# Two column pairs of the first MLP product in full, an alternating norm and split, one weight pool for both products, and the first chunk fetched earlier

## Chip, cores and metric

The kernel runs on one core of one Trainium2 chip. The metric is the device time of one execution in microseconds (us). Engines are named as in the profile: PE is the matmul engine, PEld its weight loads, DVE the vector engine, ACT the scalar engine, POOL the GpSimd engine, and SP the queue from which most DMAs are issued.

## What is computed

One residual layer on 512 frames of width 2048, all in float32. A first part (one wide projection, attention, a spatial gating unit, a merge and an output projection) gives a new `x`. The change concerns the second part:

```
h2 = rms_norm(x, g_ff)                                     # 512 x 2048
x  = x + square(relu(h2 @ w_ff1)) @ w_ff2                  # w_ff1 2048 x 8192, w_ff2 8192 x 2048
```

## The kernel before

Every product is made in three passes (`mm3`, lines 72 to 74): each operand is split into a high part, rounded to the matmul's format by an ACT cast, and a low part, the rest, by a DVE subtraction. The three matmuls are high by high, high by low and low by high. `split_to` (lines 107 and 108) and `weight` (lines 91 to 96) do this for a tile and for a streamed piece of weights.

The order on each engine is not written out by hand: a scheduler simulates the program and fills each engine's in-order queue with whatever is ready, earlier program text first. `tc.issue_after(ins)` queues what is traced inside it behind `ins` on that engine. Tiles come from pools with a fixed number of buffers; a new tile waits until one is free. When a pool is closed and another opened in its memory, the new tiles wait for the old ones.

**Pools.** `slots` has 64 buffers of 128 x 512 floats (2 KB a partition) and holds nearly everything. `long` has 12 more of that size, `short` 6, `raws` 3 of 128 x 1024 for weights on their way. After the output projection `short` and `raws` close and `raw1` (6 buffers of 128 x 1024) opens in their place. After the first MLP product `long` and `raw1` close, and `raw2` and `more2` (6 each) open. `wpool` holds three pairs of split weight pieces at a time.

**Norm.** After the output projection the transposed rows `x2T[0..15]` (each 128 x 512) are scaled by `rstd_b` on DVE (line 662), and each of their two halves of 256 frames is split (ACT cast at line 107, DVE subtraction at line 108) into `hs["y11"]`, `hs["y12"]` (even `b`) and `hs["y21"]`, `hs["y22"]` (odd `b`), eight tiles of each.

**First product.** `w_ff1` is taken in 32 pairs of column blocks (2 x 128 columns). Pair 0 is made in full (matmuls into `f`): 16 row blocks x 2 column blocks x 2 halves x 3 passes = 192 matmuls of 256 columns, with the weights in four pieces. The other 31 pairs, `hidden(p)`, use a Strassen-like scheme with seven products instead of eight (`NAMES`: y11, y21, m7, m6, y22, m4, m5): 7 x 8 x 3 = 168 matmuls of 256 columns (into `q`). The sums of the activation blocks for m7, m6, m4 and m5 are made once by `factors` (lines 643 to 646, then split): 32 DVE sums, 32 casts and 32 subtractions of 128 x 256. The sums of the weight blocks are made for each pair in `Sums.parts`: three DVE additions (lines 173, 177 and 179) and one that a DMA accumulates (line 175, POOL's queue).

`keep_hidden(p)` squares the two tiles of a pair, makes their seven factors (four sums and seven subtractions on DVE, seven casts on ACT) and stores them in DRAM (line 681, seven stores of 256 KB). In the text it stands right behind each pair.

**Second product.** It goes through eight chunks `f` of 1024 hidden columns, that is of four pairs. For each, `fetch` loads 28 tiles of 256 KB (line 730), four for each name. The outputs are made in two halves `g`, each `strassen_tokens`: seven names x two weight pieces x 12 matmuls of 512 columns. The first piece's weight blocks (`i = 0`) come from pool `state["raw"]`, the second's from `state["more"]`. The results are added to `x2` tiles, loaded again from DRAM at line 741. The tiles of chunk `f + 1` are fetched between the names of chunk `f`; chunk 0 is fetched after the last pair.

Of the kernel before, what the change touches and what calls it, by code (L numbers as in the profile page):

```python
# [2 lines left out]

# [7 lines left out]
F32R = mybir.dt.float32r  # L11
AF = mybir.ActivationFunctionType
# [15 lines left out]
W = 512  # L28
SLOTS = 64
LONG = 12  # L30
SHORT = 6


@with_exitstack
def tile_hybrid_layer(ctx: ExitStack, tc: tile.TileContext, x, g_mix, w_in, g_q, g_k, ln_g, ln_b,
# [8 lines left out]
    small = ctx.enter_context(tc.tile_pool(name="small", bufs=8))  # L44
    slots = ctx.enter_context(tc.tile_pool(name="slots", bufs=SLOTS))
    dram = ctx.enter_context(tc.tile_pool(name="dram", bufs=1, space=bass.MemoryType.DRAM))
    first, before = ExitStack(), ExitStack()
    long = first.enter_context(tc.tile_pool(name="long", bufs=LONG))
    short = before.enter_context(tc.tile_pool(name="short", bufs=SHORT))
    raws = before.enter_context(tc.tile_pool(name="raws", bufs=3))  # L50
    ps_acc = ctx.enter_context(tc.tile_pool(name="ps_acc", bufs=5, space=bass.MemoryType.PSUM))
    ps_aux = ctx.enter_context(tc.tile_pool(name="ps_aux", bufs=3, space=bass.MemoryType.PSUM))

    def slot(name, dt=F32, pool=slots):
        return pool.tile([P, 512], dt, name=name, tag="slot")

    def acc(name):
        return ps_acc.tile([P, 512], F32, name=name, tag="acc")
# [7 lines left out]
    def f32(ap):  # L66
        return ap.bitcast(F32)


    def mm3(o, lh, rh, start, stop, **kw):  # L70

        nc.tensor.matmul(o, lhsT=lh[0], rhs=rh[0], start=start, stop=False, **kw)  # L72
        nc.tensor.matmul(o, lhsT=lh[0], rhs=rh[1], start=False, stop=False, **kw)  # L73
        nc.tensor.matmul(o, lhsT=lh[1], rhs=rh[0], start=False, stop=stop, **kw)  # L74
# [12 lines left out]
    def weight(wap, kt, c0, w=W):  # L87

        ck = CK * W // w
        raw = state["raw"].tile([P, ck, w], F32, name="w_raw", tag="w_raw")  # L90
        state["load"] = nc.sync.dma_start(
            out=raw, in_=wap[kt * P:(kt + ck) * P, c0:c0 + w].rearrange("(k p) c -> p k c", p=P))
        hi = wpool.tile([P, ck, w], F32R, name="w_hi", tag="w_piece", bufs=6)
        nc.scalar.copy(out=hi, in_=raw)  # L94
        lo = wpool.tile([P, ck, w], F32R, name="w_lo", tag="w_piece", bufs=6)
        nc.vector.tensor_tensor(out=lo, in0=raw, in1=f32(hi), op=ALU.subtract)  # L96
        return hi, lo

    def split(src, name, scale=None, pool=slots):

        hi, lo = slot(name + "_hi", F32R, pool), slot(name + "_lo", F32R, pool)
        split_to(hi, lo, src, scale)
        return hi, lo

    def split_to(hi, lo, src, scale=None):
        if scale is None:
            nc.scalar.copy(out=hi, in_=src)  # L107
            nc.vector.tensor_tensor(out=lo, in0=src, in1=f32(hi), op=ALU.subtract)  # L108
        else:
            nc.scalar.activation(out=hi, in_=src, func=AF.Copy, scale=scale)  # L110
            nc.vector.scalar_tensor_tensor(out=lo, in0=src, scalar=scale, in1=f32(hi),
                                           op0=ALU.mult, op1=ALU.subtract)
# [199 lines left out]
    def hT_of(k):  # L312

        if k == len(hT):
            t = aux("xT")
            for tb in range(NTB):
                nc.tensor.transpose(out=t[:, tb * P:(tb + 1) * P], in_=xq[tb, k], identity=ident)
            hT.append(split(t, "hT", gT[:, k:k + 1], long if k < LONG // 2 else short if k < (LONG + SHORT) // 2 else slots))
        return hT[k]

    def scale_of_x():
# [309 lines left out]
    rstd2 = rsqrt(ms2, 4, "rstd2")  # L631
    flush()
    along(rstd2, rstd_b)
    before.close()
    state["raw"] = first.enter_context(tc.tile_pool(name="raw1", bufs=6))


    def factors(ys, act, k):
# [11 lines left out]
    def halves(src, pool=slots):  # L650

        t = slot("ys", F32R, pool)
        split_to(t[:, :HS], t[:, HS:], src)
        return t

    def sides(t):
        return t[:, :HS], t[:, HS:]

    hs = {}
    for b in range(KT):  # L660
        y = x2T[b]
        nc.vector.tensor_tensor(out=y, in0=y, in1=rstd_b, op=ALU.mult)
        for half in range(2):
            name = "y" + "12"[b % 2] + "12"[half]
            far = name == "y11" or name == "y21" and b // 2 < LONG - KT // 2
            hs[name, b // 2] = halves(y[:, half * HS:(half + 1) * HS], long if far else slots)

    GROUP = 4
    chunks = DFF // (GROUP * 2 * P)
# [11 lines left out]
            nc.sync.dma_start(out=store[p // GROUP][i, p % GROUP], in_=f32(ys[name, 0]))  # L681


    o = [acc("f1") for _ in range(2)]
    for kt in range(0, KT, 4):
        hi, lo = weight(w_ff1[0], kt, 0, 2 * P)
        for c in range(2):
            for k in range(4):
                a = [part[:, k, c * P:(c + 1) * P] for part in (hi, lo)]
                for half in range(2):  # L690
                    name = "y" + "12"[k % 2] + "12"[half]
                    mm3(o[c][:, half * HS:(half + 1) * HS], a, sides(hs[name, (kt + k) // 2]),
                        kt + k + half == 0, kt + k == KT - 1, skip_group_check=True)
    act = []
    for c in range(2):
        t = slot("relu")
        nc.scalar.activation(out=t, in_=o[c], func=AF.Relu)
        act.append(t)
    for k in range(KT // 2):
        factors(hs, x2T[2 * k:2 * k + 2], k)  # L700
    keep_hidden(0, act)
    rhs = {name: [sides(hs[name, k]) for k in range(KT // 2)] for name in NAMES}

    def hidden(p):

        act = [slot("relu"), slot("relu")]
        a11, a12, a21, a22 = (act[c][:, half * HS:(half + 1) * HS] for c in range(2) for half in range(2))

        def evac(name, o):
            for a, sign in {"y11": [(a11, 1.0)], "m7": [(a22, 1.0)], "m6": [(a21, -1.0)],  # L710
                            "y22": [(a12, 1.0)]}.get(name, []):
                nc.scalar.activation(out=a, in_=o, func=AF.Copy, scale=sign)  # L712
            for a, op in {"y21": [(a11, ALU.add)], "m4": [(a21, ALU.add)],
                          "m5": [(a22, ALU.subtract), (a12, ALU.add)]}.get(name, []):
                nc.vector.tensor_tensor(out=a, in0=a, in1=o, op=op)

        strassen_columns(w_ff1[0], p * 2 * P, rhs, evac)
        for a in act:
            nc.scalar.activation(out=a, in_=a, func=AF.Relu)
        keep_hidden(p, act)  # L720

    for p in range(1, DFF // (2 * P)):
        hidden(p)

    def fetch(f, name):

        ts = []
        for p in range(GROUP):
            t = slot("ys", F32R)
            nc.sync.dma_start(out=f32(t), in_=store[f][NAMES.index(name), p])  # L730
            ts.append(sides(t))
        return ts

    first.close()
    second = [ctx.enter_context(tc.tile_pool(name=n, bufs=6)) for n in ("raw2", "more2")]
    state["raw"], state["more"] = second
    lhs = {name: fetch(0, name) for name in NAMES}
    for tb in range(NTB):
        for j in range(D // W):
            t = slot("x2")  # L740
# [53 lines left out]
```

## Time and profile before

| | |
|---|---|
| median of 3 runs | 2550.4 us (2548.84 to 2552.09) |
| the profiled execution | 2549.47 us, of which the span of the trace is 2547.8 us |
| PE busy | 2485.3 us, 98% |
| DVE busy | 1608.8 us, 63% |
| ACT busy | 1041.3 us, 41% |
| POOL busy | 205.1 us, 8% |
| mean granted PE clock | 0.988 of full speed |

The page's first part gives each engine's busy time. A matmul counts as busy until its modelled end, so neighbours overlap. The second part cuts the span into 40 equal slices of 63.7 us. In later views a stretch is given by its ends in microseconds from the start of the span.

### The profile page before, as it was taken

How to read it: one execution, taken by the hardware profiler on the slowest of the kernel's cores; microseconds unless marked ns; L12 is line 12 of the kernel's file. 1: busy time of each engine (PE TensorE's matmuls, PEld its weight loads, DVE VectorE, ACT ScalarE, POOL GpSimd, SP SyncE). 2: the span in 40 equal slices, each digit the busy share in tenths (PEclk: the TensorE clock that was granted, in tenths of full speed). 3: DMA queues.
4: the chain of work that ended last, by engine and by line, in shares of the span. 5: the costliest groups of instructions: out<-in, count | busy, mean ns of one | idle time of the engine just before them, and what ended most of it. 6: DMA issues, size and time to landing. Idle time of an engine off the chain costs nothing. (4 is left out here: it accounts for less than half of the span.)

```text
span 2547.8 us, 35037 instructions
## 1 busy us (share of the span) xinstructions
PE 2485.3 (98%) x13634; PEld 2165.9 (85%) x13634; DVE 1608.8 (63%) x2116; ACT 1041.3 (41%) x1517; POOL 205.1 (8%) x186
## 2 busy tenths in 40 slices
PE   8999999999999999999789999999997999999999
PEld 7888888888888888888679999999996788888887
DVE  4555463332335333322788888888875988888887
ACT  4333332222223222222456666666663333333333
POOL 0212110000111010100000000000000000000000
PEclk9999999999999999999889999999998999999999
DMA  5332323333333333344368878888889988767763
GB/s 174 91 86 73 91 67 99 95 96 99 116 92 99 100 99 97 128 143 134 87 168 217 223 214 221 229 228 220 223 231 359 299 253 247 221 209 230 249 178 96
DMA packets 343159, 419.15 MB, mean 165 GB/s; under 512 B 17056, under 2 KB 180944, under 8 KB 342992
## 3 DMA queue, kind: packets, MB, share of 16 engines
q1 hardware_dynamic: 302048, 383.87, 46.6%
q0 software_dynamic: 40944, 33.03, 9.1%
q8 instruction: 107, 1.75, 0.3%
q14 instruction: 60, 0.49, 0.1%
HBM read 349.72 MB, written 67.11 MB: 164 GB/s over the span
## 5 line engine op out<-in xcount | busy, mean ns | idle before, releaser
L107 ACT CAST w_hi<-w_raw 128x1024 fp32r<-128x1024 f32 x441 | 464.5, 1054 | 616.4 <-PE q L73 561.0
L96 DVE TENSOR_TENSOR w_lo<-w_raw,w_hi 128x1024 fp32r<-128x1024 f32 x212 | 263.1, 1241 | 606.2 <-ACT w_hi L94 583.9
L108 DVE TENSOR_TENSOR w_lo<-w_raw,w_hi 128x1024 fp32r<-128x1024 f32 x441 | 538.7, 1222 | 166.1 <-ACT w_hi L107 165.8
L94 ACT CAST w_hi<-w_raw 128x1024 fp32r<-128x1024 f32 x212 | 223.0, 1052 | 683.7 <-PE ga L73 99.6
L72 PE MATMUL q<-ys,w_hi 128*128 128x256 f32 x1736 | 493.0, 285 | 7.3 <-ACT relu L712 3.6
L73 PE MATMUL q<-ys,w_hi 128*128 128x256 f32 x1736 | 492.7, 285 | 6.8 <-DVE ys L108 6.8
L74 PE MATMUL q<-ys,w_lo 128*128 128x256 f32 x1736 | 488.4, 284 | 0.6 <-DVE w_lo L108 0.6
L73 PE MATMUL q<-w_lo,ys 128*128 128x512 f32 x896 | 350.3, 391 | 3.0 <-DVE w_lo L108 3.0
L74 PE MATMUL q<-w_hi,ys 128*128 128x512 f32 x896 | 350.0, 391 | 0.0
L72 PEld LDWEIGHTS q<-ys,w_hi 128*128 128x128 f32 x1736 | 329.1, 190 | 9.0 <-ACT ys L107 4.3
L73 PEld LDWEIGHTS q<-ys,w_hi 128*128 128x128 f32 x1736 | 329.1, 190 | 8.2 <-DVE ys L108 8.1
L72 PE MATMUL q<-w_hi,ys 128*128 128x512 f32 x896 | 315.3, 391 | 17.3 <-DMA ys<-store 16.2
L74 PEld LDWEIGHTS q<-ys,w_lo 128*128 128x128 f32 x1736 | 327.1, 190 | 0.8 <-DVE w_lo L108 0.8
L72 PEld LDWEIGHTS q<-w_hi,ys 128*128 128x128 f32 x896 | 168.9, 189 | 54.4 <-DMA ys<-store 17.1
L73 PEld LDWEIGHTS q<-w_lo,ys 128*128 128x128 f32 x896 | 169.0, 189 | 39.2 <-DVE w_lo L108 4.1
L74 PEld LDWEIGHTS q<-w_hi,ys 128*128 128x128 f32 x896 | 169.0, 189 | 35.1
L175 POOL DMA_DIRECT2D w_raw<-in_w_ff_dram x63 | 86.5, 1373 | 1368.8 <-DVE w_raw L173 659.2
L755 DVE TENSOR_TENSOR x<-x,q 128x512 f32<-128x512 f32 x256 | 167.8, 681 | 10.8 <-PE q L74 7.0
L72 PE MATMUL gb<-hT_hi,w_hi 128*128 128x512 f32 x256 | 100.3, 392 | 0.2 <-DVE gb L454 0.2
L72 PE MATMUL xo<-w_hi,mT_hi 128*128 128x512 f32 x256 | 100.5, 393 | 0.0
L72 PE MATMUL ga<-hT_hi,w_hi 128*128 128x512 f32 x256 | 100.4, 392 | 0.0
L73 PE MATMUL ga<-hT_lo,w_hi 128*128 128x512 f32 x256 | 100.0, 391 | 0.0
(213 smaller groups left out, 4023.8 us busy)
## 6 DMA issues: line engine op xcount, KB each, us to landing
w_raw<-in_w_ff_dram SPq DMA_DIRECT2D x256, 512.0 KB, 4.9
w_raw<-in_w_in_dram SPq DMA_DIRECT2D x144, 512.0 KB, 3.8
store<-ys SPq DMA_DIRECT2D x224, 256.0 KB, 4.9
ys<-store SPq DMA_DIRECT2D x224, 256.0 KB, 5.4
w_raw<-in_w_ff_dram POOLq DMA_DIRECT2D x63, 512.0 KB, 7.0
w_raw<-in_w_out_dram SPq DMA_DIRECT2D x32, 512.0 KB, 3.7
w_raw<-in_w_oa_dram SPq DMA_DIRECT2D x16, 512.0 KB, 3.6
w_raw<-in_w_ob_dram SPq DMA_DIRECT2D x16, 512.0 KB, 3.7
```

The costliest lines, as they stand in the source:

```text
L72: nc.tensor.matmul(o, lhsT=lh[0], rhs=rh[0], start=start, stop=False, **kw)
L73: nc.tensor.matmul(o, lhsT=lh[0], rhs=rh[1], start=False, stop=False, **kw)
L74: nc.tensor.matmul(o, lhsT=lh[1], rhs=rh[0], start=False, stop=stop, **kw)
L94: nc.scalar.copy(out=hi, in_=raw)
L96: nc.vector.tensor_tensor(out=lo, in0=raw, in1=f32(hi), op=ALU.subtract)
L107: nc.scalar.copy(out=hi, in_=src)
L108: nc.vector.tensor_tensor(out=lo, in0=src, in1=f32(hi), op=ALU.subtract)
L175: nc.gpsimd.dma_start(out=self.w21, in_=self.blocks[1, 1], accum_op=ALU.add)
L755: nc.vector.tensor_tensor(out=a, in0=a, in1=o, op=op)
```

## The change

- Pairs 0 and 1 are made in full (`PLAIN = 2`); `factors` stands behind both in the text. Thirty pairs are left for the seven-product scheme.
- `keep_hidden` of pairs 0 and 1 is moved behind pair 2; from there on each pair's stands behind that pair, as before.
- The scaling of `x2T[b]` is queued on DVE behind the last subtraction of `x2T[b - 2]`.
- `raws` now has six buffers and stays open to the end; it serves as `state["raw"]` in every stage. `short` is gone. Three pairs of split input tiles (`hT` 6 to 8) that lay in `short` lie in three of these buffers.
- `long` alone closes behind the first product, and `more` opens in its place.
- `lhs`, the 28 fetches of chunk 0, stands ahead of the last `keep_hidden` in the text, where it stood behind it and behind the pools' change.

```diff
-    short = before.enter_context(tc.tile_pool(name="short", bufs=SHORT))
-    raws = before.enter_context(tc.tile_pool(name="raws", bufs=3))
+    raws = ctx.enter_context(tc.tile_pool(name="raws", bufs=6))
...
+            if LONG // 2 <= k < LONG // 2 + RAWH:
+                both = raws.tile([P, 2, W], F32R, name="hT_both", tag="w_raw")
+                parts = both[:, 0, :], both[:, 1, :]
+                split_to(*parts, t, gT[:, k:k + 1])
...
-    before.close()
-    state["raw"] = first.enter_context(tc.tile_pool(name="raw1", bufs=6))
...
+    order = []
     for b in range(KT):
         y = x2T[b]
-        nc.vector.tensor_tensor(out=y, in0=y, in1=rstd_b, op=ALU.mult)
+        with tc.issue_after(order[b - 2].ins) if b > 1 else nullcontext():
+            nc.vector.tensor_tensor(out=y, in0=y, in1=rstd_b, op=ALU.mult)
...
+        order.append(state["lo"])
...
+    PLAIN = 2
+    acts = []
+    for p in range(PLAIN):
+        o = [acc("f1") for _ in range(2)]
+        for kt in range(0, KT, 4):
+            hi, lo = weight(w_ff1[0], kt, p * 2 * P, 2 * P)
...
+        acts.append(act)
     for k in range(KT // 2):
         factors(hs, x2T[2 * k:2 * k + 2], k)
-    keep_hidden(0, act)
...
-        keep_hidden(p, act)
-
-    for p in range(1, DFF // (2 * P)):
-        hidden(p)
+        return act
...
+    pairs = DFF // (2 * P)
+    for p in range(PLAIN, pairs):
+        acts.append(hidden(p))
+        if p == pairs - 1:
+            lhs = {name: fetch(0, name) for name in NAMES}
+        while acts:
+            keep_hidden(p + 1 - len(acts), acts.pop(0))
+
     first.close()
-    second = [ctx.enter_context(tc.tile_pool(name=n, bufs=6)) for n in ("raw2", "more2")]
-    state["raw"], state["more"] = second
-    lhs = {name: fetch(0, name) for name in NAMES}
+    state["more"] = ctx.enter_context(tc.tile_pool(name="more", bufs=6))
```

## Rows read from the trace of the kernel before

**Rows 1.** The page, its 40 slices: PE's busy tenths, PE's granted clock.

```profile
PE   8999999999999999999789999999997999999999
PEclk9999999999999999999889999999998999999999
```

**Rows 2.** PE's waits over the span: what it waited for, us, times, longest.

```profile
PE q L72 <- DMA ys<-store: 16.2, 2, 15.5
PE f L73 <- DVE ys L108: 6.9, 1, 6.9
PE q L73 <- DVE ys L108: 6.8, 5, 1.7
```

**Rows 3.** Busy time by stretch: length, engines' busy us, PE clock, DMA share, GB/s.

```profile
1218.90:1235.10 16.20, 2.84 (x10) 2.28 (x10) 11.12 (x23) 9.16 (x29) 2.81 (x2) 0.58 0.28 37
1235.10:1259.50 24.40, 24.36 (x191) 24.36 (x192) 18.55 (x41) 6.25 (x11) 0.00 (x0) 0.93 0.08 23
1259.50:1302.40 42.90, 28.33 (x173) 24.91 (x172) 36.46 (x84) 22.79 (x52) 1.60 (x1) 0.76 0.38 104
1302.40:1907.10 604.70, 604.69 (x5040) 604.49 (x5038) 507.81 (x749) 386.63 (x659) 46.18 (x30) 1.00 0.82 222
1907.10:1922.60 15.50, 0.05 (x1) 0.05 (x1) 10.38 (x18) 6.62 (x13) 1.20 (x1) 0.62 0.99 324
1922.60:1967.20 44.60, 42.23 (x166) 33.58 (x167) 24.25 (x27) 13.69 (x13) 0.00 (x0) 0.90 1.04 376
1967.20:2009.20 42.00, 39.59 (x171) 31.57 (x171) 37.34 (x41) 14.67 (x15) 4.81 (x4) 1.00 1.06 346
2009.20:2542.40 533.20, 533.20 (x2353) 441.25 (x2351) 463.60 (x501) 204.78 (x194) 31.01 (x26) 1.00 0.70 212
```

**Rows 4.** DVE in order of time around the norm and the first sums.

```profile
1226.23 8.52 DVE L662 TENSOR_TENSOR x2T<-x2T,rstd_b 128x512 f32<-128x512 f32 x14
1234.67 9.47 DVE L108 TENSOR_TENSOR ys<-x2T,ys 128x256 fp32r<-128x256 f32 x28
...
1246.41 1.42 DVE L108 TENSOR_TENSOR ys<-x2T,ys 128x256 fp32r<-128x256 f32 x4
...
1254.92 1.23 DVE L108 TENSOR_TENSOR w_lo<-w_raw,w_hi 128x1024 fp32r<-128x1024 f32 x1 [4.53 <-ACT w_hi L107]
...
1286.15 0.75 DVE L108 TENSOR_TENSOR ys<-m,ys 128x256 fp32r<-128x256 f32 x2
```

**Rows 5.** PE in order of time: pair 0's stream begins, pair 1's begins.

```profile
1235.14 0.58 PE L73 MATMUL f<-ys,w_hi 128*128 128x256 f32 x1 [6.93 <-DVE ys L108]
...
1259.47 0.28 PE L72 MATMUL q<-ys,w_hi 128*128 128x256 f32 x1
```

**Rows 6.** DMA issues on SP in order of time, around the second product's start.

```profile
1891.29 2.00 SPq L167 DMA_DIRECT2D w_raw<-in_w_ff_dram  x4
...
1903.36 10.05 SPq L167 DMA_DIRECT2D w_raw<-in_w_ff_dram  x6
...
1918.09 0.98 SPq L730 DMA_DIRECT2D ys<-store  x1
...
1921.68 18.92 SPq L730 DMA_DIRECT2D ys<-store  x27
1940.96 10.48 SPq L741 DMA_DIRECT2D x<-kept  x16
1951.81 13.54 SPq L730 DMA_DIRECT2D ys<-store  x20
1965.74 3.75 SPq L167 DMA_DIRECT2D w_raw<-in_w_ff_dram  x6
```

**Rows 7.** ACT in order of time: a cast that waited for weights.

```profile
1971.90 1.05 ACT L107 CAST w_hi<-w_raw 128x1024 fp32r<-128x1024 f32 x1 [5.89 <-DMA w_raw<-in_w_ff_dram]
```

**Rows 8.** Busy time by stretch, as in Rows 3, where the DMAs were fullest.

```profile
1941.00:1952.00 11.00, 9.33 (x40) 7.20 (x39) 5.80 (x7) 2.70 (x3) 0.00 (x0) 1.00 1.05 387
```

**Rows 9.** The page's DMA issues: count, KB each, us from issue to landing.

```profile
store<-ys SPq DMA_DIRECT2D x224, 256.0 KB, 4.9
```

More of the change, by code (lines that the diff above doesn't have):

```diff
@@ L1 @@
 import collections
-from contextlib import ExitStack
+from contextlib import ExitStack, nullcontext
 import concourse.bass as bass
@@ L30 @@
 LONG = 12
-SHORT = 6
+RAWH = 3
 @with_exitstack
@@ L46, in tile_hybrid_layer @@
     dram = ctx.enter_context(tc.tile_pool(name="dram", bufs=1, space=bass.MemoryType.DRAM))
-    first, before = ExitStack(), ExitStack()
+    raws = ctx.enter_context(tc.tile_pool(name="raws", bufs=6))
+    first = ExitStack()
     long = first.enter_context(tc.tile_pool(name="long", bufs=LONG))
-    short = before.enter_context(tc.tile_pool(name="short", bufs=SHORT))
-    raws = before.enter_context(tc.tile_pool(name="raws", bufs=3))
     ps_acc = ctx.enter_context(tc.tile_pool(name="ps_acc", bufs=5, space=bass.MemoryType.PSUM))
@@ L107, in split_to @@
             nc.scalar.copy(out=hi, in_=src)
-            nc.vector.tensor_tensor(out=lo, in0=src, in1=f32(hi), op=ALU.subtract)
+            state["lo"] = nc.vector.tensor_tensor(out=lo, in0=src, in1=f32(hi), op=ALU.subtract)
         else:
@@ L317, in hT_of @@
                 nc.tensor.transpose(out=t[:, tb * P:(tb + 1) * P], in_=xq[tb, k], identity=ident)
-            hT.append(split(t, "hT", gT[:, k:k + 1], long if k < LONG // 2 else short if k < (LONG + SHORT) // 2 else slots))
+            if LONG // 2 <= k < LONG // 2 + RAWH:
+                both = raws.tile([P, 2, W], F32R, name="hT_both", tag="w_raw")
+                parts = both[:, 0, :], both[:, 1, :]
+                split_to(*parts, t, gT[:, k:k + 1])
+            else:
+                parts = split(t, "hT", gT[:, k:k + 1], long if k < LONG // 2 else slots)
+            hT.append(parts)
         return hT[k]
@@ L681, in keep_hidden @@
             nc.sync.dma_start(out=store[p // GROUP][i, p % GROUP], in_=f32(ys[name, 0]))
-    o = [acc("f1") for _ in range(2)]
-    for kt in range(0, KT, 4):
-        hi, lo = weight(w_ff1[0], kt, 0, 2 * P)
-        for c in range(2):
[L688 to L698, printed above, removed]
+    PLAIN = 2
[4 more added lines that the diff above has]
+            hi, lo = weight(w_ff1[0], kt, p * 2 * P, 2 * P)
+            for c in range(2):
+                for k in range(4):
+                    a = [part[:, k, c * P:(c + 1) * P] for part in (hi, lo)]
+                    for half in range(2):
+                        name = "y" + "12"[k % 2] + "12"[half]
+                        mm3(o[c][:, half * HS:(half + 1) * HS], a, sides(hs[name, (kt + k) // 2]),
+                            kt + k + half == 0, kt + k == KT - 1, skip_group_check=True)
+        act = []
+        for c in range(2):
+            t = slot("relu")
+            nc.scalar.activation(out=t, in_=o[c], func=AF.Relu)
+            act.append(t)
+        acts.append(act)
     for k in range(KT // 2):
         factors(hs, x2T[2 * k:2 * k + 2], k)
-    keep_hidden(0, act)
     rhs = {name: [sides(hs[name, k]) for k in range(KT // 2)] for name in NAMES}
```

## The prediction

> **What bounds the kernel now.** I read the slices first. PE is at nine tenths nearly everywhere and at full clock, except in two places: slices 20 and 21 and, later, slice 31 [rows 1]. The list of PE's waits gives them names: 16.2 us for `ys<-store`, the fetch of chunk 0, and 6.9 and 6.8 us for `ys`, the split halves and sums that DVE makes [rows 2]. The stretches then give sizes [rows 3]. From 1218.9 to 1235.1 PE waits for the norm. Pair 0 takes until 1259.5. Pair 1 takes 42.9 us, of which PE works 28.3. Thirty pairs take 604.7, that is 20.16 each, with no wait. Then PE stands for 15.5 us, and the first chunk takes 44.6 + 42.0 = 86.6 us; the other seven take 533.2, 76.17 each. So PE sets the time, and only about 65 us are to be had, at the two changes of stage. In each I look for what ends last.
>
> **Two prices for PE.** A pair is 168 matmuls, so one costs 20.16 / 168 = 0.120 us at full clock. A weight piece of the second product is 76.17 / 28 = 2.72 us.
>
> **The alternating norm.** DVE now makes 14 scalings in 8.52 us (0.609 each) before its first subtraction, at 1234.67; 28 subtractions then take 9.47 (0.338 each) [rows 4], and pair 0 starts at 1235.14 [rows 5]. With the new order two scalings come first, so the first subtraction starts at 1226.23 + 2 x 0.61 = 1227.4, and PE at about 1227.9, 7.2 us sooner. But PE then goes at DVE's pace: one `b` costs 0.609 + 2 x 0.338 = 1.285, and sixteen 20.6. The fourth `b`, with five scalings and eight subtractions, is done at 1226.23 + 5.7 = 1232.0. The 24 matmuls on the first four `b` take up to 24 x 0.24 = 5.8 us at half clock (the stretch before shows 0.58 [rows 3]), until 1233.7. The other 168 at 0.120 take 20.2: pair 0 ends near 1254. Bounds: at the soonest the last `b` comes at 1226.2 + 20.6 = 1246.8 and 30 matmuls follow, 1250.4; if the next 24 run at half clock too, 1256.8. It ended at 1259.5: I take a gain of 5.5 (2.7 to 9).
>
> **Pair 1 in full.** It costs 192 x 0.120 = 23.0 us. What goes is pair 1 as it was, 42.9 us [rows 3], with its waits for sums and its half clock. Gain 19.9, if DVE has the sums of the activations ready for pair 2's third product, m7.
>
> DVE's work from 1226.2: norm and split 20.6; five weight pieces at 1.23 [rows 4], 6.2; the 64 sums and subtractions of `factors`, of the halves' size, at 0.338, 21.6. Together 48.4, so 1274.6. Pair 2 needs DVE for some five operations of 1.23 ahead of m7: 1280.8. PE reaches pair 2 at 1254 + 23 = 1277 and m7 two products (5.8) later, 1282.8, and its last row block some 2.5 later still. That is a cover of 2 to 4.5 us. Against it: DVE's queue is in order, and a low part at its head that waits for a free buffer holds the sums behind it. It did so for 4.53 us at 1254.92 [rows 4], and the last sums came at 1286.15. Then the two postponed `keep_hidden` bring 2 x 11 x 0.338 = 7.4 us. DVE is busy 507.8 / 30 = 16.9 of 20.16 us in a pair [rows 3], and pair 2 runs without the 3.7 us of its predecessor's; so one `keep_hidden` fits there and one is left over, against pieces made up to three products (8.6 us) ahead. I take a loss of 2 us (0 if all is hidden; 10 if two waits like that at 1254.92 fall on the sums). If the cover is gone, m7 of pair 2 is late next.
>
> **The chunk fetched early.** SP issues the 28 fetches behind pair 31's stores, from 1918.09 [rows 6], when PE had been idle since 1907.1. Now 44 of the 64 slots hold activation factors, 13 the last two pairs' tiles, so seven fetches find room when pair 31 begins, and the rest as y21, m7 and m6 are used up. The first four tiles should be there before the pair ends: 15.5 us of standing go. The fetches are moved past seven stores, and what stands behind them (16 `x2` loads, 20 fetches of chunk 1, six weight loads [rows 6]) moves up with them.
>
> The first chunk also lost 86.6 - 76.2 = 10.4 us. Of this the clock is 44.6 x 0.10 = 4.5 [rows 3], which goes with the idle time; the rest is small waits. But the DMAs are full here: share 1.05, 387 GB/s [rows 8]. From 1891.3 on, up to the last six weight loads, SP and POOL issue 2 + 3.5 + 3 + 7 + 4 + 5 + 3 + 1 = 28.5 MiB (14 stores and two accumulating loads included), 29.9 MB or 77 us at 387 GB/s, and the cast that needed the end of them waited until 1971.90 [rows 7]. With one pool for both products the loads can begin as in any pair, at best 8 us sooner: 1883 + 77 = 1960, and 1962.3 with cast (1.05) and subtraction (1.23). PE would begin `g = 1` at 1907.1 + 38.1 = 1945.2; three pieces of it are loaded early, so it misses the fourth at 1953.4. If the order on SP stays, PE stands for about 9 us there; if the six weight loads pass the 20 fetches (5.2 MB, 13.5 us), for none; if the DMAs start no sooner, for 21. I take 6, so 15.5 + 10.4 - 6 = 20 us gained (5 to 26).
>
> [...]
>
> **Edits at no cost.** Six `raws` buffers, three of them taken by `hT`, leave three for the weights of the first part, as before; PE waits for none there (slices 2 to 19 [rows 1]), and at the start at worst three loads of 0.5 MB pass the `x` loads, 4 us, at best they come as much sooner. I take 0. Where the cover is lost, the second slice shows it.
>
> **The sum.** 5.5 + 19.9 - 2 + 20 = 43.4. The profiled execution took 2549.47, so 2506.1; the median is 0.9 above it: **2507 us**. The bounds together: 2.7 + 19.9 - 10 + 5 = 17.6 (2533) and 9 + 19.9 + 26 = 54.9 (2495.5).
>
> **The rivals.**
>
> *A, the DMAs keep the second gain.* SP's order puts chunk 0 late, or the full DMAs move PE's stand to `g = 1`: 23.4 us from the first place, 0 to 10 from the second, 2517 to 2527. For it: share 1.05 over 100 us [rows 3]. Against: seven free slots and 28 fetches with no other condition.
>
> *B, DVE keeps the first gain.* The sums are late in spite of pair 1: 10 us more lost, or more while the backlog lasts, 2515 to 2527. For it: the wait at 1254.92, and 84% of DVE taken in each pair. Against: between 1235.1 and 1302.4 DVE was busy for 18.6 + 36.5 of 67.3 us [rows 3], so 12 are to spare.
>
> *C, slower: the slots.* If the scheduler lets the 28 fetches take slots as soon as chunk 0 is stored, some 27 pairs run without spare slots, and a pair's tiles wait for the landing of the stores before, 4.9 us [rows 9]: 27 x 4.9 = 132 us, about 2640. It decides from 43.4 / 27 = 1.6 us a pair. [...] Against it: seven slots stood free in all 30 pairs, and no tile of chunk 0 was fetched into them before its turn [rows 6].
>
> *D, no change:* the fetches stay in place and DVE's order eats the rest. Both places would have to fail; neither depends on the other.
>
> **Chances.** Forecast (2496 to 2516) 0.66; A 0.13; B 0.12; more gain than the bounds 0.02; D 0.02; C 0.05. The range 2495 to 2530 leaves out C, D and little of A and B. About 0.2% (5 us) is what a measurement of this kernel can tell from none: faster 0.93, within 0.02, slower 0.05.
>
> **What would show it.** Pair 0's first L73 near 1228 and its end near 1254. Pair 2's first matmul near 1277, its m7 without waits on `ys`. The thirty pairs still 20.16 each; one or two longer ones at the beginning would be the backlog. No hole at the end of pair 31, PE's clock at 1.00 there. In `g = 0` to `g = 1` of chunk 0, PE's only wait, on w_hi or w_lo behind a weight DMA. I am wrong if pairs in the middle are longer than 20.2, if L730 still stands behind the last stores, or if chunk 0 takes over 95 us.

## The result and the profile after

The changed kernel takes 2531.9 us (median of 4 runs, 2528.42 to 2533.67) where the kernel before takes 2551.1 beside it: a ratio of 0.9924, 95% interval 0.9907 to 0.9942. The direction was right; of the 43.4 us that were forecast, 19.2 came by the medians. The profiled execution took 2531.66 us (span 2530.0), 17.8 less than before, and the accounts below are of profiled executions.

Line numbers have moved: the three matmuls of a product are L71 to L73, low parts L95 and L107, the sums of `factors` L646 to L649, the relu of the pairs in full L706, fetches L736, `x2` loads L753, the addition onto `x2` L767.

First the slices of the changed kernel, PE's busy tenths and its granted clock; they answer to [rows 1].

```profile
PE   8999999999999999999989999999997999999999
PEclk9999999999999999999989999999998999999999
```

Of the weak spot at slices 20 and 21 only slice 21 is left; that at slice 31 is still there. PE's waits in the changed kernel (us, times, longest), which answer to [rows 2]:

```profile
PE q L71 <- DVE x L767: 6.8, 1, 6.8
PE q L72 <- DVE ys L107: 6.7, 5, 1.7
PE q L71 <- DMA ys<-store: 4.7, 1, 4.7
...
PE q L71 <- ACT ys L106: 2.7, 2, 1.4
...
PE q L71 <- ACT relu L721: 2.0, 1, 2.0
```

The norm's 6.9 us are gone, the store's 16.2 have become 4.7. The five short waits on `ys`, which the sums make, stand as they were: 6.7 after 6.8. And one is new: 6.8 us for an addition onto `x2`. The stretches of the changed kernel, with the columns of [rows 3], say where:

```profile
1222.80:1250.60 27.80, 27.80 (x219) 27.73 (x219) 22.44 (x49) 13.24 (x34) 0.00 (x0) 0.94 0.20 58
1250.60:1271.00 20.40, 20.40 (x172) 20.40 (x171) 9.57 (x10) 7.85 (x11) 1.73 (x1) 1.00 0.30 53
1271.00:1326.00 55.00, 42.36 (x278) 38.72 (x277) 53.14 (x116) 34.73 (x78) 3.11 (x2) 0.82 0.58 173
1326.00:1899.00 573.00, 572.91 (x4765) 572.10 (x4764) 480.89 (x707) 365.17 (x621) 44.26 (x29) 1.00 0.83 224
1899.00:1903.70 4.70, 0.02 (x1) 0.02 (x1) 2.50 (x3) 1.51 (x3) 0.00 (x0) 0.94 1.10 274
1903.70:1952.30 48.60, 40.08 (x159) 31.71 (x160) 27.50 (x37) 16.47 (x21) 0.00 (x0) 0.87 1.05 388
1952.30:1991.00 38.70, 38.67 (x171) 31.65 (x170) 35.82 (x40) 14.67 (x14) 4.59 (x4) 1.00 1.06 358
1991.00:2524.00 533.00, 533.00 (x2353) 441.49 (x2352) 464.93 (x502) 204.73 (x194) 31.22 (x27) 1.00 0.70 213
```

Both pairs in full run without a hole (1222.8 to 1271). Then PE works 42.4 of 55 us at clock 0.82: pair 2 stands where pair 1 stood. In the second of these rows DVE, whose sums PE is about to wait for, works only 9.57 of 20.4 us. Its order of time there (start, length, instruction, idle time before it and what ended it) is this:

```profile
1252.05 1.23 DVE L95 TENSOR_TENSOR w_lo<-w_raw,w_hi 128x1024 fp32r<-128x1024 f32 x1 [4.58 <-ACT w_hi L93]
...
1259.93 1.23 DVE L107 TENSOR_TENSOR w_lo<-w_raw,w_hi 128x1024 fp32r<-128x1024 f32 x1 [2.92 <-ACT w_hi L106]
1265.69 1.22 DVE L107 TENSOR_TENSOR w_lo<-w_raw,w_hi 128x1024 fp32r<-128x1024 f32 x1 [4.53 <-ACT w_hi L106]
1266.94 1.23 DVE L178 TENSOR_TENSOR w_raw<-w_raw 128x1024 f32<-128x1024 f32 x1
1268.09 0.42 DVE L646 TENSOR_TENSOR m<-x2T 128x256 f32<-128x256 f32 x1
...
1296.96 1.42 DVE L107 TENSOR_TENSOR ys<-m,ys 128x256 fp32r<-128x256 f32 x4
```

The first sum, L646, begins at 1268.09 although its operands were there when the norm ended near 1247; the last of the sums' low parts ends at 1298.4. The first sum stands behind weight parts of pairs 1 and 2 (L95 and L107), and those of pair 2 wait for a cast that itself waits for PE to finish with a buffer. ACT shows these casts:

```profile
1258.85 1.05 ACT L106 CAST w_hi<-w_raw 128x1024 fp32r<-128x1024 f32 x1 [4.36 <-PE f L72]
1264.61 1.05 ACT L106 CAST w_hi<-w_raw 128x1024 fp32r<-128x1024 f32 x1 [4.71 <-PE f L72]
```

Before, the same sequence ended in a first sum at 1257.3; [rows 4] has its low part that waited 4.53.

PE in the changed kernel, at the points that answer to [rows 5] and at the begin of the second product:

```profile
1222.38 0.50 PE L71 MATMUL f<-ys,w_hi 128*128 128x256 f32 x2 [1.94 <-ACT ys L106]
...
1270.29 0.28 PE L71 MATMUL q<-ys,w_hi 128*128 128x256 f32 x1
...
1897.28 0.73 PE L71 MATMUL q<-w_hi,ys 128*128 128x512 f32 x2
...
1903.68 0.79 PE L71 MATMUL q<-w_hi,ys 128*128 128x512 f32 x1 [4.74 <-DMA ys<-store]
...
1930.78 0.80 PE L71 MATMUL q<-w_hi,ys 128*128 128x512 f32 x1 [6.84 <-DVE x L767]
```

SP's issues in the changed kernel, which answer to [rows 6], and the addition that PE waited for on DVE:

```profile
1873.60 10.54 SPq L166 DMA_DIRECT2D w_raw<-in_w_ff_dram  x7
...
1887.29 0.32 SPq L736 DMA_DIRECT2D ys<-store  x1
...
1892.48 1.00 SPq L736 DMA_DIRECT2D ys<-store  x2
...
1895.71 22.42 SPq L736 DMA_DIRECT2D ys<-store  x25
...
1922.56 2.57 SPq L753 DMA_DIRECT2D x<-kept  x3
```

```profile
1930.03 1.41 DVE L767 TENSOR_TENSOR x<-x,q 128x512 f32<-128x512 f32 x2 [7.67 <-DMA x<-kept]
```

The fetches do begin before pair 31 ends, but 25 of 28 go out in one block from 1895.71, 1.6 us before the end. Ahead of the first of them SP spends 10.54 us on seven weight loads of the second product; of SP's waits from 1870 to 1900, 10.0 us are of weight loads for buffers that DVE was still reading. The first `x2` tile, which the first addition needs, is issued behind the fetches at 1922.56. The product m6 adds onto y11's PSUM bank, and PE stood for 6.84 us until DVE had taken y11 out.

**An account that closes.** For every run I take three numbers from PE's rows in order of time. *Start* is the first matmul of the pairs in full. *Excess* is the time from there to the end of pair 31 less the matmuls themselves: 23.0 for a pair in full, 20.16 for another (the prices of the prediction). *Chunk 0* is the time from the end of pair 31 to the start of the last matmul, less 533.2 for the seven later chunks [rows 3]; so a later chunk that became longer would count in it.

| kernel | median us | ratio, 95% interval | start | first sum | excess | chunk 0 |
|---|---|---|---|---|---|---|
| before | 2551.1 | | 1227.4 | 1257.3 | 31.7 | 101.8 |
| after | 2531.9 | 0.9924 [0.9907, 0.9942] | 1222.4 | 1268.1 | 24.0 | 93.9 |
| relu_late | 2519.7 | 0.9882 [0.9868, 0.9897] | 1222.8 | 1246.3 | 9.9 | 94.4 |
| plain1 | 2533.2 | 0.9937 [0.9922, 0.9951] | 1226.9 | 1256.0 | 22.7 | 94.5 |
| x2_ahead | 2530.8 | 0.9921 [0.9904, 0.9937] | 1222.9 | 1269.2 | 24.6 | 92.2 |
| fetch_late | 2534.8 | 0.9941 [0.9926, 0.9955] | 1222.7 | 1268.2 | 21.7 | 98.0 |
| no_alt | 2537.1 | 0.9944 [0.993, 0.9959] | 1222.9 | 1276.1 | 28.3 | 94.6 |
| c1_after | 2522.7 | 0.9891 [0.9874, 0.9907] | 1223.0 | 1268.3 | 21.4 | 84.2 |
| combo | 2509.6 | 0.9837 [0.9822, 0.9852] | 1223.8 | 1248.3 | 11.1 | 83.4 |
| plain3 | 2524.4 | 0.9895 [0.988, 0.9909] | 1223.7 | 1267.9 | 12.7 | 93.6 |
| rstd_first | 2530.7 | 0.9922 [0.9907, 0.9937] | 1224.0 | 1253.2 | 22.9 | 95.6 |
| combo3 | 2514.1 | 0.9854 [0.9838, 0.9871] | 1222.9 | 1248.8 | 12.5 | 84.8 |
| combo3_spread | 2505.0 | 0.982 [0.9806, 0.9833] | 1224.0 | 1248.7 | 1.8 | 84.8 |
| combo_spread | 2511.0 | 0.9845 [0.9832, 0.9858] | 1222.9 | 1247.6 | 11.4 | 85.0 |

From before to after: 5.0 at the start; 31.7 - 24.0 less the 2.9 by which the second pair in full is dearer, 4.8; 7.9 in chunk 0. Together 17.7, and the profiled executions differ by 17.8. Excess scatters by some 3 us between profiles of kernels that are equal in the first product (after, x2_ahead, fetch_late, c1_after: 21.4 to 24.6), so single differences of that size say nothing.

### The profile page after: what moved, and what is told of

Its sections match the earlier page's. It is cut to its first block, busy times and chain, and to the rows that moved or that the text cites. A ratio compares the mean times of both kernels' runs of the same rounds, so it can differ in the third digit from the quotient of the medians.

```text
span 2530.0 us, 35066 instructions
## 1 busy us (share of the span) xinstructions
PE 2487.1 (98%) x13658; PEld 2168.7 (86%) x13658; DVE 1598.7 (63%) x2106; ACT 1036.9 (41%) x1510; POOL 204.5 (8%) x185
## 3 DMA queue, kind: packets, MB, share of 16 engines
q8 instruction: 107, 1.75, 0.3%
## 4 chain that ended last, share of the span: by engine, by line
PE 94%; DVE 2%; DMA 2%; issue 1%; ACT 1%; POOL 0%; SPq 0%; DVEq 0%; POOLq 0%
PE q L71 17%; PE q L72 17%; PE q L73 17%; PE xo L73 2%; PE xo L71 2%; PE xo L72 2%; PE gb L71 2%; PE gb L72 2%; PE gb L73 2%; PE ga L71 2%; PE ga L72 2%; PE ga L73 2%; PE v L71 1%; PE v L73 1%; PE v L72 1%
## 5 line engine op out<-in xcount | busy, mean ns | idle before, releaser
L95 DVE TENSOR_TENSOR w_lo<-w_raw,w_hi 128x1024 fp32r<-128x1024 f32 x216 | 267.9, 1240 | 597.8 <-ACT w_hi L93 593.7
L107 DVE TENSOR_TENSOR w_lo<-w_raw,w_hi 128x1024 fp32r<-128x1024 f32 x434 | 530.0, 1222 | 150.9 <-ACT w_hi L106 150.7
L72 PE MATMUL q<-ys,w_hi 128*128 128x256 f32 x1680 | 477.3, 285 | 6.7 <-DVE ys L107 6.7
L71 PE MATMUL q<-ys,w_hi 128*128 128x256 f32 x1680 | 477.6, 285 | 5.3 <-ACT ys L106 2.7
L73 PE MATMUL q<-ys,w_lo 128*128 128x256 f32 x1680 | 472.9, 284 | 0.6 <-DVE w_lo L107 0.6
L72 PE MATMUL q<-w_lo,ys 128*128 128x512 f32 x896 | 349.8, 390 | 0.8 <-DVE w_lo L107 0.8
L73 PE MATMUL q<-w_hi,ys 128*128 128x512 f32 x896 | 349.7, 390 | 0.0
L72 PEld LDWEIGHTS q<-ys,w_hi 128*128 128x128 f32 x1680 | 324.7, 193 | 8.2 <-DVE ys L107 8.1
L71 PEld LDWEIGHTS q<-ys,w_hi 128*128 128x128 f32 x1680 | 324.5, 193 | 7.3 <-ACT ys L106 4.1
L71 PE MATMUL q<-w_hi,ys 128*128 128x512 f32 x896 | 314.8, 391 | 12.5 <-DVE x L767 6.8
L73 PEld LDWEIGHTS q<-ys,w_lo 128*128 128x128 f32 x1680 | 322.7, 193 | 0.8 <-DVE w_lo L107 0.8
L71 PEld LDWEIGHTS q<-w_hi,ys 128*128 128x128 f32 x896 | 168.9, 189 | 49.5 <-DVE x L767 7.8
L72 PEld LDWEIGHTS q<-w_lo,ys 128*128 128x128 f32 x896 | 169.0, 189 | 36.5 <-DVE w_lo L107 1.5
L73 PEld LDWEIGHTS q<-w_hi,ys 128*128 128x128 f32 x896 | 168.8, 188 | 35.1
L767 DVE TENSOR_TENSOR x<-x,q 128x512 f32<-128x512 f32 x256 | 167.9, 681 | 17.8 <-PE q L73 8.2
L71 PE MATMUL xo<-w_hi,mT_hi 128*128 128x512 f32 x256 | 100.5, 393 | 0.0
L73 PE MATMUL xo<-w_hi,mT_lo 128*128 128x512 f32 x256 | 99.9, 391 | 0.0
L72 PE MATMUL xo<-w_lo,mT_hi 128*128 128x512 f32 x256 | 99.7, 389 | 0.0
L176 DVE TENSOR_TENSOR w_raw<-w_raw 128x1024 f32<-128x1024 f32 x62 | 75.8, 1223 | 10.4 <-DMA w_raw<-in_w_ff_dram 9.3
```

Of the source, the lines that this page charges most:

```text
L107: state["lo"] = nc.vector.tensor_tensor(out=lo, in0=src, in1=f32(hi), op=ALU.subtract)
L176: nc.vector.tensor_tensor(out=self.c, in0=self.a, in1=self.w22, op=ALU.add)
```

## The experiments

**1. relu_late: the sums ahead of the second relu.** The edit is to the text only; no instruction is added.

```diff
     for p in range(PLAIN):
...
+        if p == 1:
+            for k in range(KT // 2):
+                factors(hs, x2T[2 * k:2 * k + 2], k)
         act = []
         for c in range(2):
             t = slot("relu")
...
-    for k in range(KT // 2):
-        factors(hs, x2T[2 * k:2 * k + 2], k)
```

> Edit: the sums of the activations stand in the program text ahead of the relu of the second pair in full, so the two relu tiles of that pair ask for their slots behind the tiles of the sums. Nothing else differs. Theory 1 (the sums were held back by the turn in which slots are given: in the changed kernel the first sum began at 1268.09, directly behind that relu at 1267.61, with DVE busy only half of 1244 to 1268): the first sum now begins right behind the norm's last subtraction, 1245 to 1249, pair 2 loses 2 to 8 us instead of 22.1, and the time is 2512 to 2519 us. Theory 2 (DVE's own load, weight parts at 1.23 us each between the sums, makes them late): the sums still end after 1290, pair 2 and those behind it still lose over 15 us, and the time is 2525 to 2533 us.

Measured: 2519.7 us. DVE in relu_late, in order of time:

```profile
1245.62 0.76 DVE L107 TENSOR_TENSOR ys<-x2T,ys 128x256 fp32r<-128x256 f32 x2
1246.29 0.42 DVE L646 TENSOR_TENSOR m<-x2T 128x256 f32<-128x256 f32 x1
...
1250.96 1.23 DVE L95 TENSOR_TENSOR w_lo<-w_raw,w_hi 128x1024 fp32r<-128x1024 f32 x1 [3.58 <-ACT w_hi L93]
1252.10 0.42 DVE L648 TENSOR_TENSOR m<-x2T,m 128x256 f32<-128x256 f32 x1
```

The first sum follows the norm's last subtraction, 21.8 us sooner than in after. Two stretches over the same 22 us, the first of after, the second of relu_late (DVE is the third pair of numbers):

```profile
1246.00:1268.00 22.00, 22.00 (x185) 22.00 (x184) 9.86 (x10) 6.68 (x10) 1.73 (x1) 1.00 0.36 73
```

```profile
1246.00:1268.00 22.00, 22.00 (x186) 22.00 (x185) 18.11 (x39) 11.35 (x24) 1.73 (x1) 1.00 0.36 73
```

DVE's 12.1 idle us (in after the waits of 4.58, 2.92 and 4.53 make up 12.0 of them) become 3.9, and the excess falls from 24.0 to 9.9. Theory 1 holds, 0.7 us outside its range: what is left stands in pair 2 still, waits of 0.2 to 1.6 us on `ys` from 1277 on, where DVE now is full (17.99 of 18 us busy from 1282 to 1300). The last two rows of the DVE fence show the old mechanism again, a low part at the head of the queue that waits 3.58 us with a sum behind it.

What this shows is that the place of two relu instructions in the text decided where the sums stood in DVE's queue. The sums stayed behind pair 1's weight parts in the text, so their rank against those isn't the reason. That it is the slots (relu and sums take tiles from one pool, in the order of the text) fits every run here but was not tried apart from the order. On the chip the sums do not wait for the relu itself: in plain1 (experiment 2) the first sum begins at 1256.04 and the second relu ahead of it in the text only at 1256.20. What was decided is the order of DVE's queue, when the program was built.

**2. plain1: one pair in full, all else as changed.**

```diff
-    PLAIN = 2
+    PLAIN = 1
```

> Edit: only one pair in full, as before the change, with the alternating norm, the one weight pool and the early fetch kept. Theory 1 (sums wait for the relu of the last pair in full, so a second one moves the wait by one pair and covers nothing): the first Strassen pair still loses about 22 us, directly behind the relu; the pair itself is 23.0 - 20.2 = 2.9 us cheaper; the first weight sums stand again ahead of the reciprocal root on DVE and POOL, so the norm's factors are ready about 5 us later: 2531.7 - 2.9 + 5 = 2534 us (2530 to 2538). Theory 2 (the second pair in full covers the sums, as predicted, and the loss in pair 2 has another cause): the 20 us come back in pair 1 on top of it, 2545 to 2556 us.

Measured: 2533.2 us, theory 1. The excess is 22.7 where two pairs in full have 24.0. The second pair in full, for which 19.9 us had been forecast, brought 1.3 (2533.2 - 2531.9), which the spread of the runs hardly tells from nothing, although PE starts 4.5 us sooner with it. That start is a matter of the queues ahead of the norm. POOL in plain1 shows it:

```profile
1219.62 1.73 POOL L174 DMA_DIRECT2D w_raw<-in_w_ff_dram  x1 [180.15 <-ACT x2T L629]
1220.73 1.69 POOL L253 TENSOR_TENSOR rstd<-ms,mhalf 128x4 f32<-128x4 f32 x1
```

The accumulating load of the first Strassen pair is issued ahead of the reciprocal root. In after that pair comes later, and the root stands alone on POOL:

```profile
1217.81 1.02 POOL L253 TENSOR_TENSOR rstd<-ms,mhalf 128x4 f32<-128x4 f32 x1 [178.61 <-DMA kept<-x]
```

**3. rstd_first: plain1 with that queue mended.**

```diff
-        nc.vector.tensor_copy(out=r_b, in_=rp)
+        state["r_b"] = nc.vector.tensor_copy(out=r_b, in_=rp)
...
-                nc.vector.tensor_tensor(out=self.a, in0=self.w11, in1=self.w21, op=ALU.add)
+                with tc.issue_after(state["r_b"].ins):
+                    nc.vector.tensor_tensor(out=self.a, in0=self.w11, in1=self.w21, op=ALU.add)
```

> Edit: plain1 (one pair in full) with one order more: the first sum of weight blocks of the first Strassen pair (DVE, 1.23 us, and with it the accumulating load behind it on POOL, 1.73 us) only after DVE's copy of the norm's factors. Theory 1 (in the changed kernel the factors came 5.0 us sooner only because the second pair in full took these two out of the queues ahead of the reciprocal root): the factors are ready 3.5 to 5 us sooner than in plain1 (1221 to 1222.5), PE's stream begins near 1223 instead of 1227.5, the relu and the sums behind it come sooner by as much, and the time is 2528 to 2530.5 us (plain1 2533.2). Theory 2 (DVE's sums bound the first Strassen pair whatever the start): 2532 to 2535 us.

Measured: 2530.7 us, 2.5 below plain1, 0.2 above the range of theory 1. DVE's copy of the factors starts at 1221.10 (1224.97 in plain1), that is 3.9 sooner; PE's stream starts 2.9 us sooner and the first sum 2.8, because the moved sum (1.22 us) now stands between the copy and the scalings. So these two instructions account for 3.9 of the 5.0 us at the start; where the rest comes from is not shown. Of the 2.9 at the stream, 2.5 reach the end.

**4. no_alt: without the alternating order.**

```diff
-        with tc.issue_after(order[b - 2].ins) if b > 1 else nullcontext():
-            nc.vector.tensor_tensor(out=y, in0=y, in1=rstd_b, op=ALU.mult)
+        nc.vector.tensor_tensor(out=y, in0=y, in1=rstd_b, op=ALU.mult)
```

> Edit: the changed kernel without the order that makes scaling and split alternate. Theory 1 (alternation lets PE start 8 us sooner, and what follows PE's start follows it): 14 scalings, 8.5 us, stand ahead of the first subtraction again, PE's matmuls of the pairs in full begin near 1230.5 instead of 1222.9 and end near 1278, the relu and with it the first sum come 8 us later, and the time is 2537 to 2542 us. Theory 2 (DVE's sums bound pair 2 in either order): the later start is hidden, 2530 to 2534 us.

Measured: 2537.1 us, theory 1, at its lower edge. The alternation is worth 5.2 us. PE in no_alt:

```profile
1230.63 0.58 PE L72 MATMUL f<-ys,w_hi 128*128 128x256 f32 x1 [7.22 <-DVE ys L107]
```

**5. fetch_late: the fetch at its old place.**

```diff
-        if p == pairs - 1:
-            lhs = {name: fetch(0, name) for name in NAMES}
...
     state["more"] = ctx.enter_context(tc.tile_pool(name="more", bufs=6))
+    lhs = {name: fetch(0, name) for name in NAMES}
```

> Edit: the fetch of chunk 0 stands again behind the last stores, with all else of the change kept (one weight pool among it). Theory 1 (the early fetch is worth what chunk 0 gained, 8.0 us): chunk 0 takes 100 to 103 us with one hole of 13 to 16 us at its begin, and the time is 2538 to 2541 us. Theory 2 (the gain at chunk 0 came from the common weight pool, not from the fetch): 2530 to 2534 us.

Measured: 2534.8 us, between the two. Chunk 0 takes 98.0 us, with one hole of 12.35: of the 7.9 us gained there, 4.1 are the early fetch's and 3.8 are there without it. (The medians differ by 2.9 only; the excess is 2.3 smaller here, within its scatter.) SP in fetch_late suggests why:

```profile
1871.80 10.48 SPq L166 DMA_DIRECT2D w_raw<-in_w_ff_dram  x7
...
1894.35 2.98 SPq L166 DMA_DIRECT2D w_raw<-in_w_ff_dram  x2
...
1902.44 0.90 SPq L736 DMA_DIRECT2D ys<-store  x1
...
1906.21 18.00 SPq L736 DMA_DIRECT2D ys<-store  x27
```

Before, six weight loads for the second product held SP for 10.05 us at 1903.36, and the block of fetches behind them began at 1921.68 [rows 6]. With one pool the first seven loads go out from 1871.80, and the block begins at 1906.21 from its old place in the text. Pair 31 ends at different times, so I count from its end: the loads begin 23.4 us ahead of it, where they began 15.8 ahead in the kernel before (1891.29 [rows 6]); the block begins 14.6 us behind it before (1921.68 - 1907.1), 11.0 behind it in fetch_late (1906.21 - 1895.2) and 1.6 ahead of it in after (1895.71 - 1897.3). The place gave 12.6 of this. The 3.6 that are there without it fit the 3.8 in chunk 0 and the common pool, but no run takes back the pool alone, so that it is the pool is argued and not shown.

**6. x2_ahead: the tiles of `x2` that are needed first ahead of 20 tiles of chunk 0.**

```diff
+            lhs = {name: fetch(0, name) for name in NAMES[:2]}
+            load_x2((0, 1))
+            lhs.update({name: fetch(0, name) for name in NAMES[2:]})
-            lhs = {name: fetch(0, name) for name in NAMES}
...
+    load_x2((2, 3))
-    for tb in range(NTB):
-        for j in range(D // W):
-            t = slot("x2")
-            nc.sync.dma_start(out=t, in_=kept[tb, j])
-            x2[tb, j] = t
```

> Edit: the fetch of chunk 0 is cut: tiles of y11 and y21 first, then the eight x2 tiles of the first half (j = 0, 1), then the other 20 tiles of chunk 0; the other eight x2 tiles where they were. Theory 1 (the first accumulation onto x2 is late because its tiles are loaded behind 25 fetches; m6 takes over y11's bank and waits for it): the wait of 6.84 us for the evacuation of y11 goes, chunk 0 takes 87 to 90 us instead of 94.1, the time is 2525 to 2528 us. Theory 2 (the DMAs are full, so what is put first only makes another tile late): a wait of similar size stands on the tiles of m7 or on w_hi, and the time is 2530 to 2534 us.

Measured: 2530.8 us, theory 2 in number. The 6.84 us are gone, but PE in x2_ahead now waits within `g = 1` (and 3.00 and 1.75 us for fetches at the begin, where after waits 4.74):

```profile
1963.81 2.17 PE L71 MATMUL q<-w_hi,ys 128*128 128x512 f32 x4 [4.87 <-ACT w_hi L106]
```

The weights for it were issued behind 13 tiles of chunk 1. SP in x2_ahead:

```profile
1941.75 10.77 SPq L736 DMA_DIRECT2D ys<-store  x13
1952.93 1.72 SPq L166 DMA_DIRECT2D w_raw<-in_w_ff_dram  x3
```

**7. c1_after: besides that, chunk 1's tiles behind the weights of `g = 1`.**

```diff
-                if f < chunks - 1 and (i < 5 if g == 0 else i < 7):
+                if f == 0:
+                    for n in () if g == 0 else NAMES[:6] if i == 5 else NAMES[i:7]:
+                        if n not in ahead:
+                            with tc.issue_after(state["load"].ins):
+                                ahead[n] = fetch(f + 1, n)
+                elif f < chunks - 1 and (i < 5 if g == 0 else i < 7):
                     ahead[NAMES[i]] = fetch(f + 1, NAMES[i])
```

> Edit: x2 tiles of the first half ahead of 20 tiles of chunk 0 as in x2_ahead, and the tiles of chunk 1 are fetched only behind the last weight loads of g = 1 of chunk 0. Theory 1 (in x2_ahead the wait did not go but moved to g = 1, 4.87 us on w_hi at 1963.8, because 28 tiles of chunk 1, which PE needs only from about 1975, were issued ahead of those weights; with the order by need the DMAs are fast enough): no wait over 1.5 us in g = 1, chunk 0 takes 82 to 87 us (94.1 in the changed kernel), the time is 2519 to 2525 us. Theory 2 (the sum of the bytes is the limit, in any order): the wait only moves on, to the tiles of chunk 1 or the weights, and the time is 2528 to 2533 us.

Measured: 2522.7 us, theory 1. SP in c1_after:

```profile
1938.75 1.68 SPq L166 DMA_DIRECT2D w_raw<-in_w_ff_dram  x3
1940.69 22.89 SPq L736 DMA_DIRECT2D ys<-store  x24
```

The three weight loads go out 14.2 us sooner (11.1 counted from the end of pair 31), the largest wait in `g = 1` is 0.89, and chunk 0 takes 84.2 us in place of 93.9. The DMAs are as full as ever: share 1.06 at 369 GB/s over chunk 0 of c1_after (1895.2 to 1979.5), against 1.06 at 367 over 1897 to 1991 in after. At an equal rate the shorter chunk has moved fewer bytes, 31.1 MB (369 x 84.3) against 34.5. So the rate is at its level in both, and what the order decides is which bytes have to come before the chunk can end. 8 us over the 76.2 of a later chunk remain, 4.5 of them the first wait on a fetch.

**8. combo: 1 and 7 together.** No other edit.

> Edit: the sums ahead of the second relu (relu_late), x2 tiles earlier, and chunk 1's tiles behind the weights of g = 1. Theory 1 (two independent places): both gains add, 2519.7 less 7 to 12, so 2507 to 2513 us. Theory 2 (DMA-bound behind pair 31: what the first product gains, the second waits for): 2517 to 2521 us.

Measured: 2509.6 us, theory 1. The two gains alone are 12.2 and 9.1, together they give 22.3.

**9. plain3: relu_late with three pairs in full**, the sums ahead of the third relu.

```diff
-    PLAIN = 2
+    PLAIN = 3
...
-        if p == 1:
+        if p == PLAIN - 1:
```

> Edit: three pairs in full, and the sums ahead of the third pair's relu alone. Theory 1 (the 9.9 us that PE still loses in relu_late are sums that are not ready when the first Strassen pair begins; 23 us more of matmuls cover them): the first Strassen pair loses under 4 us, the third pair costs 2.9 us more than a Strassen pair, 2514 to 2518 us. Theory 2 (each pair in full adds as much work to DVE as it gives time, weight parts and one more postponed set of tiles): the loss stays, 2521 to 2526 us.

Measured: 2524.4 us, the number of theory 2. But its trace has the cause of experiment 1: the second relu again stands ahead of the sums in the text, and the first sum begins at 1267.9, as in after. So this run didn't test its theories, and the next was made to. The excess still fell to 12.7, for the sums kept their place and PE had a third pair to work on.

**10. combo3: combo with three pairs, the sums still ahead of the second relu.**

```diff
-    PLAIN = 2
+    PLAIN = 3
```

> Edit: combo with three pairs in full, the sums still ahead of the relu of the second one (in plain3 they stood ahead of the third one's relu and behind the second's). Theory 1 (plain3 brought nothing because its sums began at 1267.9, again behind the second pair's relu, not because a third pair loads DVE): the sums begin at 1246 to 1250 and end near 1280, the first Strassen pair begins near 1293 and loses under 3 us, and the time is 2502 to 2506.5 us (combo 2509.6). Theory 2 (the third pair brings DVE as much postponed work as time): 2509 to 2514 us.

Measured: 2514.1 us, slower than combo: theory 2. Yet the sums began at 1248.8, the last one at 1285.5, and pair 3 at 1294.76 had no wait on them. What came instead, PE and then ACT in combo3:

```profile
1334.51 0.58 PE L71 MATMUL q<-ys,w_hi 128*128 128x256 f32 x1 [6.18 <-ACT relu L722]
```

```profile
1332.00 0.41 ACT L106 CAST ys<-m 128x256 fp32r<-128x256 f32 x1 [1.94 <-DVE m L647]
1333.47 0.71 ACT L106 CAST ys<-m 128x256 fp32r<-128x256 f32 x2 [1.06 <-DVE m L648]
1334.09 0.92 ACT L722 ACTIVATE relu<-q 128x256 f32<-128x256 f32 x3
```

Four `keep_hidden` at once fill DVE (19.46 of 20 us busy from 1314 to 1334). ACT's casts wait for their sums, and behind the casts, in ACT's queue, stands the emptying of a PSUM bank (L722) that PE needs.

**11 and 12. combo3_spread and combo_spread: at most two `keep_hidden` behind a pair.**

```diff
-        while acts:
+        for _ in range(len(acts) if p == pairs - 1 else min(2, len(acts))):
             keep_hidden(p + 1 - len(acts), acts.pop(0))
```

> Edit: combo3 with the postponed squares, splits and stores of the three pairs in full spread out: at most two pairs' worth per pair, in place of four at once behind the first Strassen pair. Theory 1 (combo3's sums were in time, 1248.8 to 1282.0, but four postponed sets stood ahead of an emptying of PSUM in ACT's queue: 6.18 us at 1334.51, and 1.10 at 1325.43): both waits go or fall under 1.5 us, 2514.1 less 6 to 9, so 2505 to 2508 us. Theory 2 (the postponed work is too much for DVE and ACT at any distance, it only comes later): 2511 to 2516 us.

> Edit: combo (two pairs in full) with the same spreading. Theory 1 (in combo PE waits for the sums in pair 2, 4.8 us, and the postponed sets cost only 0.16): no change, 2508 to 2511 us. Theory 2 (DVE is full from 1282 to 1300, 17.96 of 18 us, also because of three postponed sets at once): 2503 to 2507 us.

Measured: 2505.0 and 2511.0 us, theory 1 in both. Stretches of combo3_spread, in order the three pairs in full, the first Strassen pairs, and the rest of the first product:

```profile
1222.80:1294.60 71.80, 70.65 (x576) 70.65 (x577) 58.80 (x126) 38.14 (x85) 1.73 (x1) 0.97 0.27 67
1294.60:1326.00 31.40, 31.40 (x264) 31.40 (x263) 26.09 (x44) 21.49 (x40) 1.56 (x1) 1.00 0.78 224
1326.00:1879.50 553.50, 553.50 (x4612) 553.27 (x4611) 471.20 (x702) 355.30 (x611) 44.25 (x29) 1.00 0.85 231
```

PE has no hole left from 1294.6 to the end of the first product; the excess is 1.8 us. This is the fastest kernel of the study, 1.8% below before. It gets to the time that was forecast for the change, but only with five edits more: the sums' place, a third pair in full, the spreading, the early `x2` tiles and chunk 1 behind the weights.

## Why the prediction was too large

**The alternating norm (5.5 us; 2.7 to 9).** Right: 5.2 by experiment 4. The first L72 came 7.8 us sooner (1222.88 against 1230.63 in no_alt) where 7.2 had been forecast for the begin of the stream. The rest of the gain got through because the hold of the sums moved with PE's stream (first sum at 1268.1 and 1276.1).

**The start (not in the sum).** PE began at 1222.4, not 1227.9: the factors were ready 5.0 us sooner. I had taken 1226.23 [rows 4] as given, without asking what stood on POOL and DVE ahead of the reciprocal root. The change moves the first Strassen pair back by one pair in full (23.0 us) and with it two instructions out of those queues; experiment 3 shows it from the other side, for 3.9 of the 5.0.

**Pair 1 in full (19.9) less the backlog (2; 0 to 10).** This is the step that failed, in the sentence "Together 48.4, so 1274.6". It let the sums begin when DVE was free. I had named what speaks against it, the low part at the queue's head that waited 4.53 us, but priced it as one or two such waits. The hold is not one wait: it is the whole time from the end of the norm to the place where the sums stand in the queue, 1247 to 1268, and the last of their low parts came at 1298.4 where 1274.6, or 1280.8 with five weight operations of pair 2, had been forecast. That place follows the relu that stands ahead of the sums in the text, so a second pair in full moves the sums by as much as it covers: excess 22.7 with one pair, 24.0 with two. With the sums in their place the cover works (9.9), and with three pairs and the postponed work spread it is complete (1.8). Norm, pair 1 and backlog were to give 23.4 together; they gave 4.8.

**The early fetch (20; 5 to 26).** 7.9, and 3.8 of these are there without the early fetch. The common pool, to which the rows of experiment 5 point, I had counted only in the stand at `g = 1` ("at best 8 us sooner"). The step that failed here is the statement that "seven fetches find room when pair 31 begins": it begins near 1877.1 (1897.3 - 20.16), and one went out at 1887.3, two at 1892.5 and 25 from 1895.7, among and behind pair 30's stores. I had counted free slots but not what stands ahead of the fetches on SP, seven weight loads from 1873.6 to 1884.1; no run moved those apart. The hole shrank from 15.5 to 4.7 us only, and PE ran at 0.87 of its clock behind it. And 6.84 us came where I had looked for none: the `x2` loads were listed with what "moves up with them", not as something that PE needs within `g = 0`. The 6 us of standing at `g = 1` did not come in after. They came, as 4.87, as soon as the `x2` wait was taken away, some 11 us into `g = 1` (1963.81 - 4.87, where `g = 1` began 38.1 + 4.87 us before the chunk's end at 1990.6).

**The sum.** 43.4 - 18.6 - 12.1 + 5.0 = 17.7. That this is nearly the worst sum of the bounds (17.6, 2533) is luck: norm, pair 1 and backlog gave 4.8 where their bounds allow no less than 12.6 (2.7 + 19.9 - 10), the fetch was above its lower bound, and the 5.0 at the start stood in no term.

**The rivals.** A (the DMAs keep the second gain) and B (DVE keeps the first) both came true, B by the place of the sums and not by DVE's load alone, and I had priced each as if the other held its forecast; together, 2507 and at least 10 and 8 more, they give 2525 and up. C did not come: 1326 to 1899 runs without a hole.

**What stays open:** whether the slots' turn or another rule of the order puts the sums behind the relu; whether the common pool alone gave the 3.8 us of experiment 5; and the first wait on a fetch of chunk 0, 4 to 5 us in most versions here. No other place for those first tiles was tried.

## What to carry to other kernels

Work that is to be hidden has to be able to start: before its duration is set against a cover, look up what stands ahead of it in its engine's queue, and what those instructions wait for. An engine that is idle while its work is ready (DVE, 12.1 of 22 us) is the sign, and moving two instructions in the text was worth as much as two thirds of the whole change. Where DMAs are full (share 1.06 over chunk 0 here, at 367 to 369 GB/s), order the loads by when each is needed, and count the bytes that must come before the point in question. In x2_ahead the loads moved ahead took away a wait of 6.84 us and left one of 4.87 on weights, at 2530.8 us; the gain appeared only in c1_after, 2522.7 us, when chunk 1's tiles had been put behind those weights.

## What the runs showed of the hardware

- The same share of the DMAs (1.06) and nearly the same rate (367 and 369 GB/s) went with 93.9 us (after) and with 84.2 us (c1_after) for chunk 0.
- The row of POOL's reciprocal root of 128x4 reads 1.02 us alone (after) and 1.69 behind the issue of an accumulating load, whose own row reads 1.73 (plain1). The two rows overlap by 0.62, and from the end of the issue the root took 1.07: what the rows show is a root that comes later, not one that is slower.
- PE's granted clock over one stretch, 1222 to 1246, was 1.00 in relu_late and 0.90 in combo, whose text is the same up to there: the eight matmuls of the factors, behind a wait of 1.21 us in both, took 1.13 us in the one and 2.01 in the other. So a difference of 1 to 2 us at such a place can't be put down to an edit.
- m6, which by the scheme of the seven products accumulates onto the PSUM bank that holds y11, started 6.84 us late in after: PE's row at 1930.78 names DVE's addition onto `x2` as what it waited for. That addition, which takes y11 out, began at 1930.03 after waiting 7.67 us for its `x2` tile.
